# Turning the larger probability blocks of layer 1 on VectorE and by DMA, with TensorE's order tied

## The chip, the cores and the metric

The kernel runs on one core of a Trainium2 chip. A core has TensorE (PE, the matrix engine, whose weight loads the profile lists apart as PEld), VectorE (DVE), ScalarE (ACT), GpSimd (POOL) and SyncE (SP), which here issues nearly all DMAs. Each engine runs its own instructions in order and waits for the others by semaphores. The metric is the device time of one execution in microseconds (us).

## The reference

One step of a two-layer streaming encoder, on 512 prompt rows and 32 sample rows. Layer 0 is an RWKV-7 mixer, layer 1 differential attention with 12 heads of width 128; each layer has one input projection, memory attention beside the mixer, a SiLU gate and an output projection. The part that matters is layer 1's prompt attention, done for each head in four blocks of 128 queries, where a query sees the keys of its own block and of those before it:

```python
def probs(qa, ka):
    s = jnp.einsum('bqhd,bkhd->bhqk', qa, ka).astype(jnp.float32) * DF_HD ** -0.5
    return jax.nn.softmax(jnp.where(mask, s, NEG_INF), axis=-1)

attn = probs(q1, k1) - lam * probs(q2, k2)
return jnp.einsum('bhqk,bkhd->bqhd', attn.astype(v_all.dtype), v_all)
```

## The kernel before

**The projections set the beat.** All 544 rows lie turned in SBUF, split into a high and a low part (`hh`, `hl`). Each 128 columns of a weight matrix are a block: the weights arrive as two loads (`raw`), ScalarE rounds them to `whi`, VectorE takes the rest as `wlo`, and TensorE runs 48 matmuls into `ps_g`: two halves of 272 rows, eight k-parts, and for each `hh,whi`, `hl,whi`, `hh,wlo`. `block` writes these 48 in order and, ahead of the matmul with a given index, takes a step of other work. In `groups`, four heads make a group, and there are three groups; each head has a K, a Q and a V block, then gate and memory blocks follow.

**A head's steps.** `diff_head` is a generator; `groups` places its steps in its own V block, in the next head's K, Q and V blocks, and in the gate block after the fourth head. `turned(k)` and `turned(v)` turn keys and values within 32 rows on VectorE (`kt`, `vb`) and store them by DMA; `vscr` is the DRAM scratch of the values, and `fetched` loads it back in order as `vt`. `scores(t)`, for query block t, runs the `ps_s` matmuls, takes the maxima on VectorE (`snm`), the exponentials on ScalarE (`pt`) and combines both softmaxes on VectorE. `probs(t)` turns the t + 1 key blocks of `pt` on TensorE into `ps_aT`, which ScalarE copies to `aT`. `weighted(t)` multiplies `aT` with `vt` into `ps_o`, t + 1 matmuls of two passes each. `taken` copies `ps_o` to `ot` on VectorE and squares it on ScalarE. `diff_end` ends a group: the sample rows' result `ps_os`, its norm on VectorE (`os`), its turn `ps_osT` and each head's turn `ps_oT`.

**What sets the order.** The instructions are written in program order, and a scheduler then lays out each engine's order by readiness. `Queue.tie` can bind a queue's instructions to the program's order; in the kernel before it does so only in a part of layer 0 (`self.ordered`), so in layer 1 the scheduler places TensorE's instructions too.

Of the kernel before, what the change touches and what calls it, by code (L numbers as in the profile page):

```python
# [97 lines left out]
class Queue:  # L98


    def __init__(self, trunk, engine):
        self.trunk, self.engine, self.last = trunk, engine, None

    def __getattr__(self, name):
        issue = getattr(self.engine, name)
# [3 lines left out]
class Trunk:  # L109
# [12 lines left out]

    def tie(self, queue, ins):

        if self.ordered:
            if queue.last is not None:
                self.order(ins, queue.last)
            queue.last = ins
        return ins
# [1654 lines left out]
    def layer1(self):  # L1784
# [7 lines left out]
        with ExitStack() as ctx:  # L1792
            with ExitStack() as c2:
                self.dfp = p = self.pool("df", 1, ctx=c2)
                m1 = c2.enter_context(ExitStack())
                mp = self.pool("mem1a", 1, ctx=m1, side="right")

                nlam = self.nlam
                self.vscr = [self.dp.tile([TP, P], F32, name=f"vscr{i}") for i in range(2)]
                self.qs = [p.tile([P, P], F32, name=f"qs{i}") for i in range(2)]  # L1800
                for t in self.qs:
                    nc.gpsimd.memset(t[:], 0.0)  # L1802
                self.kz = [p.tile([P, 2, T], F32R, name=f"kz{i}") for i in range(2)]
                for t in self.kz:
                    for m in range(2):
                        r = slice(64 - 64 * m, P - 64 * m)
                        nc.gpsimd.memset(t[r, m, :].bitcast(F32), 0.0)
                pe, early = [], iter(order[:MADE])

                def aside():  # L1810
                    if pe:
                        made.update({g: self.gated(g, *self.fetch(pe[0], g)) for g in islice(early, 2)})

                def free():
                    m1.close()
                    pe.append(self.pool("wo1e", 1, ctx=ctx, side="right"))

                self.groups(w, p, mp, nlam, aside, free)
            p = self.pool("wo1", 1, ctx=ctx)
            fw = p.tile([P, D], F32, name="fw")  # L1820
            self.se.dma_start(fw[:], a["final_norm_w"].unsqueeze(0).to_broadcast([P, D]))
            sums = p.tile([P, T], F32, name="sums")
            ys = [p.tile([P, D], F32, name=f"fy{i}") for i in range(5)]
            rows = [P] * 4 + [TS]

            def transposed(s, pool, tag, tiles=range(5)):

                for i in tiles:
                    ps = pool[i].tile([P, 512], F32, tag=tag[i], name="ps_f")
                    for k in range(4):  # L1830
                        c = min(i * P, T - P)
                        self.te.transpose(ps[:, k * P : k * P + P], self.x1[:, 4 * s + k, c : c + P], self.ident[:])
                    yield i, slice(P - rows[i], P), ps

            def consume(k, ps, v):
                x = self.x1[:, k, v]
                if k == KT - 1:
                    cuts = (TH, 3 * P, TP, T) if v.start else (0, TH)
                    for c, e in zip(cuts, cuts[1:]):
                        x = self.x1[:, k, c:e]  # L1840
                        self.ve.tensor_tensor(x, ps[:, c - v.start : e - v.start], x, ALU.add)
                        self.ae.activation(last[:, c:e], x, AF.Square)
                    if not v.start:
                        pn.append(begun((0, 1), self.psx, "x"))
                        pn.append(begun((2, 3, 4), self.psc, "c"))
                    finish((2, 3, 4) if v.start else (0, 1))
                    return
                self.ve.tensor_tensor(x, ps, x, ALU.add)
                self.square_sums((k, x, v), p, sums)
                if k == 3 and v.start:  # L1850
                    for i, n, pf in transposed(0, [self.psm] * 5, "mmmmm"):
                        self.ve.tensor_tensor(ys[i][n, :512], pf[n, :], fw[n, :512], ALU.mult)

            last = p.tile([P, T], F32, name="last")
            rs, invd, epsd = (p.tile([P, n], F32, name=f"fr{i}") for i, n in enumerate((5, 1, 5)))
            nc.gpsimd.memset(invd[:], 1.0 / D)
            nc.gpsimd.memset(epsd[:], EPS / P)
            pn = []

            def begun(tiles, pool, tag):  # L1860

                ps = pool.tile([P, 512], F32, tag=tag, name="ps_n")
                self.te.matmul(ps[:, : len(tiles)], self.ones[:], epsd[:, : len(tiles)], start=True, stop=False)
                for j, i in enumerate(tiles):
                    c = min(i * P, T - P)
                    self.te.matmul(ps[:, j : j + 1], sums[:, c : c + P], invd[:], start=False, stop=False)
                return ps


            def finish(tiles):  # L1870

                ps = pn.pop(0)
                for j, i in enumerate(tiles):
                    c = min(i * P, T - P)
                    self.te.matmul(ps[:, j : j + 1], last[:, c : c + P], invd[:], start=False, stop=i == tiles[-1])
                v = slice(tiles[0], tiles[-1] + 1)
                self.rsqrt(rs[:, v], ps[:, : len(tiles)], p, f"tm_t{tiles[0]}")
                for i, n, pf in transposed(1, [self.psm, self.psm, self.psc, self.psm, self.psg], "mmcmg", tiles):
                    r = rs[n, i : i + 1]
                    self.ve.scalar_tensor_tensor(ys[i][n, 512:], pf[n, :], r, fw[n, 512:], ALU.mult, ALU.mult)  # L1880
                    self.ae.activation(ys[i][n, :512], ys[i][n, :512], AF.Copy, scale=r)
                    self.se.dma_start(o[0][0, i * P : i * P + P, :] if i < 4 else o[1][0], ys[i][n, :])

            for _ in self.w_out(1, p, order, consume, o=made)[0]:
                pass
# [13 lines left out]
    def groups(self, w, p, mp, nlam, aside, free):  # L1899

        late = []
        for hg in range(3):
            gr = self.diff_group(hg, p)
            heads = [self.diff_head(gr, j, p, nlam) for j in range(4)]
            sgs, fins, prev = [], [], None
            step = lambda it, *at: [(i, lambda: next(it, None)) for i in at]

            turns = lambda it, last: step(it, 6) + step(last, 8) + step(it, 20, 36) + step(last, 40) + step(it, 47)

            def gate(c0, pieces):  # L1910
                self.gates += 1
# [4 lines left out]
            for j, (parts, it) in enumerate(heads):  # L1916
                h = 4 * hg + j
                before = step(prev, 4, 14, 24, 36) if j else late
                k, q, v = parts()
                self.block(w, MIXW + h * P, k, before)  # L1920
                if not j and hg == 2:
                    free()
                next(it)
                self.block(w, h * P, q, step(prev, 4, 40) if j else ())
                if j:
                    aside()
                if j == 3 and hg < 2:
                    mem = [self.mem_turn(1, 2 * hg + i, mp) for i in range(2)]
                    for _ in range(2):
                        next(mem[0][1])  # L1930
                self.block(w, 2 * MIXW + h * P, v, turns(it, prev if j else iter(())))
                prev = it
            end = self.diff_end(gr, nlam)
            fin = lambda j, at: (at, lambda: end.send((j, sgs[j])))
            g0 = 4 * hg * P
            sgs.append(gate(g0, step(prev, 4, 14, 24, 36)))
            if hg == 2:
                sgs.append(gate(g0 + P, step(prev, 4, 28, 40, 45)))
                aside()
                sgs.append(gate(g0 + 2 * P, step(end, 2, 10, 18) + [fin(0, 22), fin(1, 36)]))  # L1940
                sgs.append(gate(g0 + 3 * P, [fin(2, 16)]))
                fin(3, 0)[1]()
                break
            (st0, m0), (st1, m1) = mem
            for st, h in ((st0, 2 * hg), (st1, 2 * hg + 1)):
# [43 lines left out]
    def diff_head(self, gr, j, p, nlam):  # L1989
# [65 lines left out]
        def probs(t):  # L2055
# [4 lines left out]
            st["aT", t] = p.tile([P, 512], F32, tag="aT", name="aT", bufs=3)  # L2060
            self.ae.copy(st["aT", t][:, :n], ps[:, :n])

        def weighted(t):
            aT = st["aT", t]
            if t == 0:
                st["po"] = self.psx.tile([P, 4, P], F32, tag="x", name="ps_o")
            for i in range(t + 1):
                self.te.matmul(st["po"][:, t, :], aT[:, i * P : i * P + P], st["vt"][:, i, :], start=i == 0, stop=i == t)

        def taken():  # L2070
            ot = st["ot"]
# [5 lines left out]
        def steps():  # L2077
# [39 lines left out]
            yield  # L2117
            scores(3)
            yield
            probs(2)  # L2120
            yield
            for t in range(3):
                weighted(t)
            self.se.dma_start(o[5][0, 0, :, h, :].rearrange("(i p) d -> p i d", p=P), st["vt"][:])
            probs(3)
            yield
            weighted(3)
            yield
# [139 lines left out]
```

## Time and profile before

| | |
|---|---|
| median of 3 runs | 1360.98 us (1359.95 to 1361.36) |
| the profiled execution, its own time | 1360.13 us |
| its span, first to last instruction | 1358.4 us |
| granted clock of TensorE, mean | 0.998 |
| DMA, mean over the span | 107 GB/s |

By stretches of the span, the first column giving start:end in us, then the length, the busy time and number of instructions of PE, PEld, DVE, ACT and POOL, the granted clock, the busy share of the DMA engines and GB/s:

```profile
712.00:797.00 85.00, 83.60 (x676) 82.44 (x674) 51.17 (x108) 37.58 (x82) 2.53 (x6) 1.00 0.57 154
797.00:1250.00 453.00, 450.67 (x3512) 437.54 (x3511) 312.61 (x862) 252.82 (x769) 6.34 (x6) 1.00 0.44 112
1250.00:1358.40 108.40, 100.26 (x804) 99.48 (x802) 46.50 (x89) 28.36 (x57) 7.02 (x4) 0.97 0.27 84
```

The heads of layer 1 fill the middle row. In a timeline a row is start, length, engine, line, operation, written tile <- read tiles, shapes and count, and in brackets the idle time before it with what ended it. Every row has line 106, a helper's, so tiles tell the rows apart. Matmuls are pipelined: a single one's length is longer than the distance between two starts.

### The profile page before, as it was taken

How to read it: one execution, taken by the hardware profiler on the slowest of the kernel's cores; microseconds unless marked ns; L12 is line 12 of the kernel's file. 1: busy time of each engine (PE TensorE's matmuls, PEld its weight loads, DVE VectorE, ACT ScalarE, POOL GpSimd, SP SyncE). 2: the span in 40 equal slices, each digit the busy share in tenths (PEclk: the TensorE clock that was granted, in tenths of full speed). 3: DMA queues.
4: the chain of work that ended last, by engine and by line, in shares of the span. 5: the costliest groups of instructions: out<-in, count | busy, mean ns of one | idle time of the engine just before them, and what ended most of it. 6: DMA issues, size and time to landing. Idle time of an engine off the chain costs nothing. (4 is left out here: it accounts for less than half of the span.)

```text
span 1358.4 us, 31641 instructions
## 1 busy us (share of the span) xinstructions
PE 1328.2 (98%) x11725; PEld 1271.8 (94%) x11725; DVE 945.2 (70%) x2373; ACT 804.1 (59%) x2252; POOL 370.4 (27%) x833
## 2 busy tenths in 40 slices
PE   8999999999999999999999999999999999999997
PEld 6988899999999998988999999999999999999997
DVE  5766778878888888666754677775577747777443
ACT  5766777877787776656433466654466536665222
POOL 2128668666776667600000000000000001002000
PEclk9999999999999999999999999999999999999999
DMA  6452322333223332432565574543354424443322
GB/s 223 144 139 68 86 59 67 85 94 82 72 81 87 79 84 65 116 107 81 160 158 144 142 200 110 130 119 93 95 127 111 113 79 108 119 107 103 94 79 73
DMA packets 330964, 145.54 MB, mean 107 GB/s; under 512 B 129865, under 2 KB 319826, under 8 KB 330810
## 3 DMA queue, kind: packets, MB, share of 16 engines
q1 hardware_dynamic: 330746, 143.51, 39.5%
q8 instruction: 92, 1.51, 0.5%
q14 instruction: 62, 0.51, 0.1%
q10 hardware_dynamic: 64, 0.02, 0.0%
HBM read 113.87 MB, written 26.06 MB: 103 GB/s over the span
## 5 line engine op out<-in xcount | busy, mean ns | idle before, releaser
L106 PE MATMUL ps_g<-hh,wlo 128*128 128x272 f32 x1808 | 537.9, 298 | 1.1 <-DVE wlo L106 1.0
L106 PE MATMUL ps_g<-hh,whi 128*128 128x272 f32 x1808 | 534.3, 296 | 0.9 <-DVE ats L106 0.7
L106 PE MATMUL ps_g<-hl,whi 128*128 128x272 f32 x1808 | 533.1, 296 | 0.9 <-DVE hl L106 0.7
L106 PEld LDWEIGHTS ps_g<-hh,whi 128*128 128x128 f32 x1808 | 341.6, 189 | 5.3 <-issue 0.9
L106 PEld LDWEIGHTS ps_g<-hl,whi 128*128 128x128 f32 x1808 | 341.3, 189 | 3.6 <-DVE hl L106 1.8
L106 PEld LDWEIGHTS ps_g<-hh,wlo 128*128 128x128 f32 x1808 | 341.2, 189 | 2.9 <-DVE wlo L106 1.8
L106 DVE TENSOR_TENSOR wlo<-raw,whi 128x512 fp32r<-128x512 f32 x314 | 213.6, 692 | 120.2 <-ACT whi L106 116.3
L106 ACT CAST whi<-raw 128x512 fp32r<-128x512 f32 x314 | 188.7, 619 | 121.4 <-PE ps_g L106 69.8
L868 POOL TENSOR_TENSOR tm<-u,m 102x84 f32<-102x84 f32 (+23 forms) x341 | 147.6, 433 | 115.8 <-DMA m<-sc 67.4
L870 POOL TENSOR_TENSOR u<-u,tm 102x84 f32<-102x84 f32 (+23 forms) x341 | 152.8, 448 | 26.6
L106 PE MATMUL ps_g<-hi,wlo 128*128 128x272 f32 x512 | 148.0, 289 | 0.9 <-DVE wlo L106 0.9
L106 PE MATMUL ps_g<-hi,whi 128*128 128x272 f32 x512 | 147.8, 289 | 0.0
L106 PE MATMUL ps_g<-lo,whi 128*128 128x272 f32 x512 | 147.6, 288 | 0.0
L1339 POOL TENSOR_TENSOR lo<-og,hi 128x544 fp32r<-128x544 f32 x8 | 13.2, 1652 | 386.0 <-ACT hi L106 385.5
L106 PEld LDWEIGHTS ps_g<-hi,wlo 128*128 128x128 f32 x512 | 96.5, 188 | 1.5 <-DVE wlo L106 1.4
L106 PEld LDWEIGHTS ps_g<-hi,whi 128*128 128x128 f32 x512 | 96.7, 189 | 0.0
L106 PEld LDWEIGHTS ps_g<-lo,whi 128*128 128x128 f32 x512 | 96.5, 188 | 0.0
L106 ACT ACTIVATE pt<-ps_s,snm 128x128 f32<-128x128 f32 (+3 forms) x96 | 50.1, 526 | 59.9 <-DVE snm L106 59.7
L106 DVE SCALAR_TENSOR_TENSOR SB<-ps_c,dl,sd 64x64 f32<-64x64 f32 x168 | 47.4, 282 | 26.4 <-PE ps_c L106 21.9
L106 ACT COPY sv<-ps_c 64x64 f32<-64x64 f32 x192 | 39.5, 206 | 32.8 <-PE ps_c L106 30.9
L1802 POOL MEMSET qs<- 128x128 f32 x2 | 0.3, 204 | 187.0 <-PE ps_g L106 187.0
L106 ACT ACTIVATE sg<-ps_g 128x272 f32<-128x272 f32 x64 | 25.2, 393 | 41.2 <-PE ps_g L106 38.2
(393 smaller groups left out, 2522.7 us busy)
## 6 DMA issues: line engine op xcount, KB each, us to landing
raw<-in_rw_in_dram SPq DMA_DIRECT2D x114, 256.0 KB
raw<-in_df_in_dram SPq DMA_DIRECT2D x112, 256.0 KB
raw<-in_w_out_dram SPq DMA_DIRECT2D x64, 256.0 KB
oscr<-sg SPq DMA_DIRECT2D x16, 272.0 KB
lo<-oscr SPq DMA_DIRECT2D x16, 272.0 KB
m<-sc SPq DMA_DIRECT2D x33, 128.0 KB
raw<-in_w_mem_v_dram SPq DMA_DIRECT2D x16, 256.0 KB
kh<-kh SPq DMA_DIRECT2D x24, 136.0 KB
```

What stands on the lines that cost most here:

```text
L106: return lambda *a, **k: self.trunk.tie(self, issue(*a, **k))
L868: nc.gpsimd.tensor_tensor(tm[:, :n, :wd], u3[:, :n, kx : kx + 1].to_broadcast(sh), m3[:, kx : kx + 1, kx + 1 :].to_broadcast(sh), ALU.mult)
L870: nc.gpsimd.tensor_tensor(u3[:, :n, kx + 1 :], u3[:, :n, kx + 1 :], tm[:, :n, :wd], ALU.add)
L1339: (self.nc.gpsimd if g % 2 and self.o1 else self.ve).tensor_tensor(lo[:], t, hi[:].bitcast(F32), ALU.subtract)
L1802: nc.gpsimd.memset(t[:], 0.0)
```

## The change

For the first three heads of each group, `probs(2)` and `probs(3)` are replaced by `moved(2)` and `moved(3)`: VectorE turns `pt` within 32 rows and 32 columns, writing with steps of 3 or 4 elements; one DMA stores the result to a DRAM scratch (`ascr`), and four DMAs load it into place, so that key block i of the result is the columns i, i + t + 1, and so on. `weighted` reads its stationary operand with that step. The fourth head keeps `probs`. Two tiles that are not yet in use in that stage (`og` 8 and 9 as output of the turn, 10 and 11 as result) hold the data. The steps move: `weighted(0)` and `(1)` now come at index 40 of the next head's Q block, `(2)` at 16 and `(3)` at 44 of its V block, `taken` at index 2 of the K block after it. TensorE's order in all three groups is tied to the program's.

```diff
-        if self.ordered:
+        if self.ordered or queue.tied:
...
+                self.ascr = [self.dp.tile([P, TP], F32, name=f"ascr{i}") for i in range(4)]
...
+        self.te.last, self.te.tied = None, True
...
-            turns = lambda it, last: step(it, 6) + step(last, 8) + step(it, 20, 36) + step(last, 40) + step(it, 47)
+            turns = lambda it, last: step(it, 6) + step(last, 16) + step(it, 20, 36) + step(last, 44) + step(it, 47)
...
                 before = step(prev, 4, 14, 24, 36) if j else late
+                if j > 1:
+                    before = step(heads[j - 2][1], 2) + before
...
-                self.block(w, h * P, q, step(prev, 4, 40) if j else ())
+                self.block(w, h * P, q, step(prev, 4, 30, 40) if j else ())
...
-            sgs.append(gate(g0, step(prev, 4, 14, 24, 36)))
+            sgs.append(gate(g0, step(heads[2][1], 2) + step(prev, 4, 14, 24, 36)))
...
+                self.te.tied = False
...
+        def moved(t):
+            n, pt, s = (t + 1) * P, st["pt", t], self.ascr[2 * (h % 2) + t - 2]
+            x, to = self.o1[6 + t][:, :n], self.o1[8 + t]
+            self.ve.transpose(x.rearrange("p (b c i) -> p b i c", b=4, c=TS),
+                              pt[:, 0, :n].rearrange("p (i b c) -> p b i c", b=4, c=TS))
+            self.se.dma_start(s[:, :n], x)
+            for b in range(4):
+                r, c = slice(TS * b, TS * b + TS), slice(n // 4 * b, n // 4 * b + n // 4)
+                self.se.dma_start(to[r, :n].rearrange("i (a w) -> i a w", a=4),
+                                  s[:, c].rearrange("(a i) w -> i a w", a=4))
+            st["aT", t] = to[:, :n].rearrange("p (q i) -> p i q", q=P)
...
-                self.te.matmul(st["po"][:, t, :], aT[:, i * P : i * P + P], st["vt"][:, i, :], start=i == 0, stop=i == t)
+                a = aT[:, i] if t > 1 and j < 3 else aT[:, i * P : i * P + P]
+                self.te.matmul(st["po"][:, t, :], a, st["vt"][:, i, :], start=i == 0, stop=i == t)
...
-            probs(2)
-            yield
-            for t in range(3):
+            if j == 3:
+                probs(2)
+                yield
+            else:
+                for t in (2, 3):
+                    moved(t)
+                    yield
+            for t in range(3 if j == 3 else 2):
                 weighted(t)
...
-            probs(3)
+            if j == 3:
+                probs(3)
+            else:
+                yield
+                weighted(2)
```

**TensorE in the first block of the first group.** The matmuls read `hl` while its last two k-parts are still being made; a wait for VectorE on a row with `hl` is the wait for such a part, one for ScalarE on a row with `hh` that for its high part. The order before:

```order
L106 MATMUL ps_g<-hh,whi 128x272 [waits Activation_49]
L106 MATMUL ps_g<-hh,whi 128x272
L106 MATMUL ps_g<-hl,whi 128x272
L106 MATMUL ps_g<-hh,wlo 128x272
L106 MATMUL ps_g<-hl,whi 128x272 [waits DVE_49]
```

and now, from the same row on:

```order
L106 MATMUL ps_g<-hh,whi 128x272 [waits Activation_49]
L106 MATMUL ps_g<-hl,whi 128x272 [waits DVE_49]
L106 MATMUL ps_g<-hh,wlo 128x272
L106 MATMUL ps_g<-hh,whi 128x272 [waits Activation_49]
L106 MATMUL ps_g<-hl,whi 128x272 [waits DVE_49]
```

The fifth row is the 797.47 us row of the trace before, where `hl`'s last part but one is read. Now it reads the last part, whose reader stood 19 rows further on.

**TensorE and VectorE around `weighted(0)` and the second head's softmaxes.** TensorE in the next head's Q block, before:

```order
L106 MATMUL ps_aT<-ident,pt 128x128 x4
L106 MATMUL ps_g<-hl,whi 128x272
L106 MATMUL ps_g<-hh,wlo 128x272
L106 MATMUL ps_o<-vt,aT 128x128 x6
L106 MATMUL ps_g<-hh,whi 128x272
```

and now:

```order
L106 MATMUL ps_g<-hh,wlo 128x272
L106 MATMUL ps_g<-hh,whi 128x272
L106 MATMUL ps_o<-vt,aT 128x128 x3
L106 MATMUL ps_g<-hl,whi 128x272
L106 MATMUL ps_g<-hh,wlo 128x272
```

`weighted(0)` comes two `ps_g` earlier in the block, with no turn ahead of it, and with three matmuls (blocks 0 and 1) instead of six. VectorE at the end of `scores(1)`'s softmax and at the start of `scores(3)`'s, one piece each of the difference:

```order
 L106 RECIPROCAL srs<-srs 128x2
 L106 TENSOR_TENSOR srs<-srs,nlam 128x1
+L106 COPY ot<-ps_o 128x512
 L106 TENSOR_SCALAR pt<-pt,srs 128x256
 L106 TENSOR_TENSOR wlo<-raw,whi 128x512
```

```order
 L106 SCALAR_TENSOR_TENSOR pt<-pt,srs 128x384
-L106 MEMSET ps_s 64x64 x2
+L106 MEMSET ps_s 64x64
+L106 STREAM_TRANSPOSE og_12308<-pt 128x4x3x32
+L106 MEMSET ps_s 64x64
 L106 TENSOR_REDUCE snm<-ps_s 128x1 x2
 L106 RECIPROCAL srs<-srs 128x2
```

The copy of the previous head's `ps_o` and the turn of block 2 (`og_12308` is its output) have entered VectorE's queue ahead of these softmaxes; for a group's first head there is no copy, and the turn stands behind the reduction. SyncE's queue there now:

```order
L106 DMA ascr_12326<-og_12308 128x384
L106 DMA out_dram<-kt 32x16x32
L106 DMA vt<-vscr_12323 128x4x128
L106 DMA raw<-in_df_in_dram 128x4x128
L106 DMA kh<-kh 64x544 x2
L106 DMA og_12310<-ascr_12326 32x4x96 x4
L106 DMA ascr_12327<-og_12309 128x512
L106 DMA out_dram<-vt 128x4x128
L106 DMA raw<-in_df_in_dram 128x4x128 x2
L106 DMA og_12311<-ascr_12327 32x4x128 x4
```

The rows with `ascr` are new: one store and four loads for each of the two blocks, the loads of block 2 behind `kh`, those of block 3 behind two `raw` loads.

**TensorE at a group's end.** `ps_osT` moves up by nine `ps_g`. Before, ahead of the first head's `ps_oT`:

```order
L106 MATMUL ps_osT<-ident,os 128x128
L106 MATMUL ps_g<-hh,wlo 128x272
L106 MATMUL ps_g<-hh,whi 128x272
L106 MATMUL ps_g<-hl,whi 128x272
L106 MATMUL ps_oT<-ident,ot 128x128 x4
```

Now twelve `ps_g` rows stand between `ps_osT` and `ps_oT`:

```order
L106 MATMUL ps_g<-hh,wlo 128x272
L106 MATMUL ps_g<-hh,whi 128x272
L106 MATMUL ps_g<-hl,whi 128x272
L106 MATMUL ps_osT<-ident,os 128x128
L106 MATMUL ps_g<-hh,wlo 128x272
```

In the third group `ps_os` moves up by nine `ps_g` as well, and `ps_osT` stands eight `ps_g` behind it.

More of the change, by code (lines that the diff above doesn't have):

```diff
@@ L101, in __init__ @@
     def __init__(self, trunk, engine):
-        self.trunk, self.engine, self.last = trunk, engine, None
+        self.trunk, self.engine, self.last, self.tied = trunk, engine, None, False
     def __getattr__(self, name):
```

## The prediction

> **What bounds the kernel now.** I read the page's busy times and the granted clock first, then busy time by stretch around the four heads of layer 1's first group, then TensorE's waits, then the chain and the timelines of one head.
>
> ```profile
> span 1358.4 us, 31641 instructions
> PE 1328.2 (98%) x11725; PEld 1271.8 (94%) x11725; DVE 945.2 (70%) x2373; ACT 804.1 (59%) x2252; POOL 370.4 (27%) x833
> PEclk9999999999999999999999999999999999999999
> 820.00:906.00 86.00, 85.48 (x669) 83.68 (x668) 62.02 (x168) 52.15 (x163) 0.00 (x0) 1.00 0.50 123
> ```
>
> TensorE (PE) is busy for 85.48 of 86 us there, at the full clock, and VectorE (DVE) for 62. So work taken off PE is worth its time, but only where nothing else is about to end last, and a new PE wait costs its full length. What comes nearest to that is in PE's waits from 795 to 1232 us (total, times, longest):
>
> ```profile
> PE ps_o L106 <- DMA vt<-vscr: 1.1, 3, 0.5
> PEld ps_o L106 <- DMA vt<-vscr: 2.2, 5, 0.7
> ```
>
> `weighted(0)`, the first `ps_o` matmul of a head, waits for `vt` in 8 of 12 heads. The next rows (PE, DVE, SyncE's queue, then the chain's prices) are the second head's way there.
>
> ```profile
> 836.52 0.28 PE L106 MATMUL ps_s<-kh,qp 128*128 128x256 f32 x1
> 839.65 0.17 DVE L106 RECIPROCAL srs<-srs 128x2 f32<-128x2 f32 x1 [0.76 <-ACT pt L106]
> 842.90 1.02 DVE L106 TENSOR_REDUCE snm<-ps_s 128x1 f32<-128x384 f32 x2
> 844.76 0.17 DVE L106 RECIPROCAL srs<-srs 128x2 f32<-128x2 f32 x1 [0.84 <-ACT pt L106]
> 846.38 1.29 DVE L106 TENSOR_REDUCE snm<-ps_s 128x1 f32<-128x512 f32 x2
> 848.64 0.17 DVE L106 RECIPROCAL srs<-srs 128x2 f32<-128x2 f32 x1 [0.98 <-ACT pt L106]
> 849.05 0.71 DVE L106 STREAM_TRANSPOSE kt<-k 128x512 f32<-128x512 f32 x1
> 849.79 0.32 SPq L106 DMA_DIRECT2D out_dram<-kt  x1
> 850.29 0.38 SPq L106 DMA_DIRECT2D vt<-vscr  x1
> 853.24 1.41 PEld L106 LDWEIGHTS ps_o<-vt,aT 128*128 128x128 f32 x12 [0.20 <-DMA vt<-vscr]
> 848.05 4.51 PE ps_g L106 x36
> 852.56 0.44 PE ps_aT L106 x4
> 853.25 1.59 PE ps_o L106 x12
> ```
>
> `scores(1)` starts at 836.52. The `vt` load is issued at 850.29 (13.77 us later), because SyncE issues in order and the `kt` store ahead of it waits for DVE's turn of `kt` at 849.05, which stands behind both softmaxes. PE starts `ps_o` at 853.24: 2.95 us after the issue, 16.72 us after `scores(1)`, with 0.20 us of wait. So PE's work between `scores(1)` and `weighted(0)` is already as short as the `vt` load allows. Prices: `ps_g` 4.51/36 = 0.125 us, a transpose 0.44/4 = 0.11, a `ps_o` matmul (two passes, twelve rows for six) 2 × (1.59 - 0.20)/12 = 0.23.
>
> **The transposes.** Nine heads lose 3 + 4 of them: 63 × 0.11 = 6.9 us of PE work. Every one stood ahead of `weighted(0)`, in the stretch that `vt` already sets. So I don't book the 6.9; I work out the head instead.
>
> **The heads.** For the second and third head of a group PE would now reach `weighted(0)` at 16.72 - 0.20 (wait) - 0.77 (seven transposes) - 0.25 (it moves two `ps_g` forward) + 0.93 (the four `ps_o` of the head before, which now follow `scores(1)`) = 16.43 us after `scores(1)`. The `vt` issue moves the other way. Between the two reciprocals at 839.65 and 844.76 DVE idles only 0.84 us, and that idle follows the reduction; into this stretch comes the copy of `ot`:
>
> ```profile
> L106 DVE COPY ot<-ps_o x12: 684/692/693, 833.8 to 1229.9; 128x512 f32<-128x512 f32 x12
> L106 DVE STREAM_TRANSPOSE kt<-k 128x512 f32<-128x512 f32 x12 | 8.5, 710 | 0.4
> L106 DVE STREAM_TRANSPOSE new<-k 128x32 f32<-128x32 f32 x12 | 2.5, 212 | 0.4
> ```
>
> That is 0.69. Beside it the K block itself starts 0.93 later after `scores(1)`, and with it the copy of `v` that DVE's `vb` needs; the two overlap, and I take 0.9. Then `moved(2)` stands between the memsets ahead of the reduction at 846.38: a turn of 384 columns, between 212 ns at 32 and 710 at 512, is 0.58 by straight line. Reduction, exponentials, `kt`, its store and `vt` follow in one chain, so the issue comes 1.5 later, at 15.27, and `vt` lands at 18.22: PE waits 1.8 us. Its start moves by 18.22 - 16.72 = +1.50. Behind it, up to the next `scores(1)`, six instead of ten `ps_o` matmuls and two more `ps_g` stand: -0.93 + 0.25 = -0.68. Each of the two heads: +0.82.
>
> The group's first head has no `ot` copy, and its `moved(2)` falls into the 0.98 us idle at 848.64, so its `vt` is not later:
>
> ```profile
> 825.27 0.38 SPq L106 DMA_DIRECT2D vt<-vscr  x1
> 828.56 1.50 PE L106 MATMUL ps_o<-vt,aT 128*128 128x128 f32 x12
> 897.19 0.46 SPq L106 DMA_DIRECT2D vt<-vscr  x1
> 902.67 1.50 PE L106 MATMUL ps_o<-vt,aT 128*128 128x128 f32 x12
> ```
>
> PE can start at 825.27 + 2.95 = 828.22 instead of 828.56: -0.34 - 0.68 = -1.02. In the fourth head the third's four `ps_o` come on top (+0.93); there `ps_o` came 5.5 us after the issue, so no wait forms. A group: -1.02 + 2 × 0.82 + 0.93 = +1.55; three groups **+4.7 us**.
>
> **The tied order, first block.** PE can no longer pass `hl` parts that are late:
>
> ```profile
> 797.47 0.40 PE L106 MATMUL ps_g<-hl,whi 128*128 128x272 f32 x1 [0.32 <-DVE hl L106]
> 798.36 0.65 ACT L106 CAST hh<-hn 128x544 fp32r<-128x544 f32 x1
> 799.04 0.72 DVE L106 TENSOR_TENSOR hl<-hn,hh 128x544 fp32r<-128x544 f32 x1 [0.80 <-ACT hh L106]
> ```
>
> Before, the matmul that uses the last `hl` stood 19 rows behind the one at 797.47 (19 × 0.125 = 2.4 us). Now it has that one's own row, and `hl` is ready at 799.76 whatever PE does: **+2.3 us**.
>
> **The tied order, `ps_osT`.** It moves nine `ps_g` (1.13 us) forward in each group; in the last group `ps_os` does too, and `ps_osT` stands eight `ps_g` behind it.
>
> ```profile
> 913.95 0.29 DVE L106 TENSOR_SCALAR os<-os,os 128x128 f32<-128x128 f32 x1
> 914.39 0.30 PE L106 MATMUL ps_osT<-ident,os 128*128 128x128 f32 x1
> 1076.41 0.30 PE L106 MATMUL ps_osT<-ident,os 128*128 128x128 f32 x1 [0.21 <-DVE os L106]
> 1233.48 0.16 PEld L106 LDWEIGHTS ps_os<-cv,aTs 128*32 128x32 f32 x8 [0.18 <-ACT aTs L106]
> 1237.22 0.75 DVE L106 SCALAR_TENSOR_TENSOR og<-ps_oT,dv,sg 128x512 f32<-128x512 f32 x1
> 1237.88 0.29 DVE L106 TENSOR_SCALAR os<-os,os 128x128 f32<-128x128 f32 x1
> ```
>
> DVE's rows up to `os` are the same in the first two groups. There `os` is done at 914.24 where PE would come at 913.26: +1.0; the second waited already: +1.1. In the third `ps_os` waited already (+1.1), and `os` is done at 1238.17 less the 0.66 of the `og` row that now follows it, 1237.5, where PE comes at 1233.5 + 0.7 + 8 × 0.125 = 1235.2: +2.3; grouped transposes and an earlier `ps_o` give back some 0.5. **+5.0 us.**
>
> **What costs nothing, and its cover.** ScalarE's 18 `aT` copies fall away; nobody waited for them. The `og` loads of `moved(2)` stand on SyncE's queue behind `kh`:
>
> ```profile
> 851.32 1.10 SPq L106 DMA_DIRECT2D kh<-kh  x2
> L106 SPq DMA_DIRECT2D vs<-new x12: 599/608/736, 894.3 to 1220.5; - x12
> ```
>
> With `kh` 1.5 later the four go out from 853.9 to 856.4 (0.61 each, like `vs`). None carries more than a fifth of `vt`'s bytes, so the last lands within `vt`'s 2.95 us of its issue at 855.8, by 858.7; `weighted(2)` comes 24 `ps_g` and three `ps_o` after `weighted(0)` at 854.7, at 858.4. I take no wait, for the smaller load; at worst 0.3 × 9 = 2.7 us. `raw` loads queue some 3 us later but feed blocks two further on (12 us). `moved(3)`'s turn (0.71) and the second `kt` stores hide behind PE's wait. A strided write could make `moved(2)` up to twice as long (+0.58 × 6 = +3.5) and not shorter than a plain turn; I take the plain row, the same instruction.
>
> **The sum.** 4.7 + 2.3 + 5.0 = +12.0 us on the profiled execution's 1360.13 us: 1372.1. The median of the runs is 0.85 above that execution, so 1373.0 (+0.9%).
>
> **Rivals.**
>
> *The weight loads get slow.* `weighted(2)` and `(3)` now read their stationary operand in steps of 12 and 16 bytes; nothing in the trace reads so. Nearest row:
>
> ```profile
> L106 PEld LDWEIGHTS ps_o<-vt,aT x240: 186/192/193, 828.4 to 1229.5; 128*128 128x128 f32 x120
> ```
>
> Nine heads × 7 matmuls × 2 passes = 126 passes of 0.116; at twice that, +14.6: 1387.6. Bounds 0 and 14.6; I take 0, as plain rows cost. It decides from a load that no longer fits under the matmul ahead. The Trainium skill, page "SBUF — State Buffer", section "Door 1: The DMA port swizzle", says that SBUF has 16-byte lines and needs two accesses to a line for full bandwidth, yet also calls a stride of four fp32 free: the first would make this rival true, the second not. No row here shows which.
>
> *DVE's delay does not reach `vt`.* Then a group is -1.02 - 2 × 0.68 + 0.93 = -1.45, the sum -4.4 + 7.3 = +3.0: 1364.0. Against it: DVE has no idle left ahead of 846.38.
>
> *Faster: `vt` is in time.* If `vt` were issued by 16.43 - 2.95 = 13.48 us after `scores(1)`, the 6.9 us and the 3.3 us of present waits would go: -10.2 + 7.3 = -2.9, 1358.1. It needs 0.3 us less than the trace's 13.77, where I count 1.5 more.
>
> **Numbers.** The forecast 0.57 (1366 to 1380), slow loads 0.17, no delay 0.15, faster 0.06, something else 0.05. The range 1362 to 1388 leaves out the faster case, part of the third and the far end of the first. A change under 0.2% (2.7 us) is about what a measurement of this kernel can't tell from none: faster 0.07; within, half of the no-delay case and some of the rest, 0.10; slower 0.83.
>
> **What would show it.** Right: PE and PEld waits of `ps_o` on `vt` of 1 to 2 us in two heads of three; one wait of about 2.3 us of `ps_g` on `hl` near 798 us; waits of `ps_osT` on `os` of 1, 1 and 2.3; `ps_aT` down to 57. Wrong: `vt` issued no later after `scores(1)`, waits of `ps_o` on `og`, or `ps_o` rows much apart where nothing is waited for.

## The result, and the profile after

The changed kernel takes 1385.51 us (median of 6 runs, 1382.39 to 1387.31) where the kernel before takes 1361.42 (1359.95 to 1361.92): a ratio of 1.0176 with a 95% interval of 1.0163 to 1.0189, or +24.1 us. The forecast was slower by 12.0, at 1373.0. The direction held; the size was half of what came.

The page of the kernel after (profiled execution 1387.31 us), and TensorE's waits over the span (total, times, longest):

```profile
span 1385.6 us, 31645 instructions
PE 1338.9 (97%) x11662; PEld 1281.0 (92%) x11662; DVE 962.8 (69%) x2391; ACT 796.3 (57%) x2234; POOL 371.1 (27%) x833
```

```profile
PE ps_o L106 <- DMA vt<-vscr: 8.6, 9, 1.5
PE ps_osT L106 <- DVE os L106: 4.8, 3, 2.4
PE ps_g L106 <- ACT hh L106: 1.6, 1, 1.6
PE ps_g L106 <- DVE hl L106: 1.2, 3, 0.7
PE ps_os L106 <- ACT aTs L106: 1.1, 1, 1.1
PE ps_o L106 <- DMA og<-ascr: 0.6, 2, 0.3
```

TensorE has 63 matmuls fewer and yet is busy 10.7 us longer. The waits stand where the prediction put them: `vt` (in nine heads; it named two of every three), `ps_osT` three times, `hl` and its high part `hh` in the first block; the short ones for `og` are new. They explain the idle time, not the busy time. That comes from two other rows. First, `ps_o` by its stationary operand (ns min/median/max of one):

```profile
L106 PEld LDWEIGHTS ps_o<-vt,og x126: 251/319/332, 839.8 to 1234.7; 128*128 128x128 f32 x126
L106 PEld LDWEIGHTS ps_o<-vt,aT x114: 186/192/192, 836.1 to 1251.7; 128*128 128x128 f32 x114
```

Read in steps of 12 and 16 bytes (`og`), a load takes 251 to 332 ns, read plainly (`aT`) 186 to 192. Second, the clock in the first block and at the third group's end (by stretches; the granted clock is the third column from the end):

```profile
800.00:802.00 2.00, 0.99 (x6) 0.54 (x4) 1.94 (x4) 0.23 (x1) 0.00 (x0) 1.00 0.91 270
802.00:804.00 2.00, 0.59 (x1) 0.28 (x1) 0.68 (x1) 1.16 (x3) 0.00 (x0) 0.84 0.84 258
804.00:806.00 2.00, 1.90 (x8) 1.90 (x9) 0.04 (x1) 0.39 (x1) 0.00 (x0) 0.50 0.76 208
806.00:808.00 2.00, 2.00 (x15) 2.00 (x14) 0.00 (x0) 0.00 (x0) 0.00 (x0) 0.80 0.77 270
...
1258.00:1260.00 2.00, 0.00 (x0) 0.00 (x0) 2.00 (x15) 0.00 (x0) 0.00 (x0) 1.00 0.37 107
1260.00:1262.00 2.00, 1.97 (x12) 2.00 (x13) 1.69 (x9) 0.37 (x1) 0.00 (x0) 0.69 0.00 0
1262.00:1264.00 2.00, 2.00 (x11) 2.00 (x10) 1.38 (x5) 0.40 (x1) 0.00 (x0) 0.50 0.00 0
```

TensorE idles, and just behind the idle time it runs at half clock: 8 or 11 matmuls in 2 us instead of some 16 (669 in 86 us before). PE's timeline in the first block, and the row of the third end that waits:

```profile
801.18 0.40 PE L106 MATMUL ps_g<-hl,whi 128*128 128x272 f32 x1 [0.71 <-DVE hl L106]
...
803.34 0.59 PE L106 MATMUL ps_g<-hh,whi 128*128 128x272 f32 x1 [1.64 <-ACT hh L106]
804.10 0.59 PE L106 MATMUL ps_g<-hl,whi 128*128 128x272 f32 x1 [0.17 <-DVE hl L106]
804.49 0.43 PE L106 MATMUL ps_g<-hh,wlo 128*128 128x272 f32 x1
804.72 0.43 PE L106 MATMUL ps_g<-hh,whi 128*128 128x272 f32 x1
...
806.90 0.29 PE L106 MATMUL ps_g<-hl,whi 128*128 128x272 f32 x1
807.03 0.29 PE L106 MATMUL ps_g<-hh,wlo 128*128 128x272 f32 x1
...
1260.03 0.30 PE L106 MATMUL ps_osT<-ident,os 128*128 128x128 f32 x1 [2.39 <-DVE os L106]
```

Starts are 0.23 us apart from 804.49 on and 0.13 again behind 806.90. The trace's record of the granted clock has 3.41 us at 0.5 there, worth 1.7 us, and as much behind 1260.03.

**Where the 27.2 us lie.** The two spans differ by 27.2. The start of the same instruction in both traces, subtracted, gives how far the kernel after lags at each place:

| stretch | before grows by |
|---|---|
| up to the first block of the groups (793.76 us before, 797.46 after) | +3.7 |
| first block, up to the first `scores` (16.07 us before, 20.21 after) | +4.1 |
| heads of the three groups | +4.4, +4.4, +3.7 |
| the three group ends | +1.1, +1.0, +4.5 |

The first row isn't the change's: up to there no engine's order differs, and in the 15 further profiles below that block starts between 791.8 and 795.1. In this execution a stretch of 6.83 us at half clock, at 131 us, makes 3.4 of it. The other rows, 23.2 in all, come near the 24.1 between the medians.

The first head's `ps_o`, and then the second head, as in the prediction's rows:

```profile
836.08 0.94 PE L106 MATMUL ps_o<-vt,aT 128*128 128x128 f32 x6 [0.55 <-DMA vt<-vscr]
843.89 0.28 PE L106 MATMUL ps_s<-kh,qp 128*128 128x256 f32 x1
845.88 2.10 PE L106 MATMUL ps_o<-vt,og 128*128 128x128 f32 x8 [0.34 <-DMA og<-ascr]
855.20 0.69 DVE L106 STREAM_TRANSPOSE og<-pt 128x384 f32<-128x384 f32 x1
859.72 0.36 SPq L106 DMA_DIRECT2D vt<-vscr  x1
862.82 0.94 PE L106 MATMUL ps_o<-vt,aT 128*128 128x128 f32 x6 [1.06 <-DMA vt<-vscr]
866.63 1.19 PE L106 MATMUL ps_o<-vt,og 128*128 128x128 f32 x6
872.10 2.01 PE L106 MATMUL ps_o<-vt,og 128*128 128x128 f32 x8
```

`vt` is issued 15.83 us after `scores(1)` (13.77 before) and `ps_o` starts at 18.93 (16.72 before). The eight strided passes of `weighted(3)` take 2.01 us, so 0.23 each, (2.01 - 0.40)/7; the six plain ones of 862.82 0.11, (0.94 - 0.38)/5; the six of `weighted(2)` at 866.63 0.16, (1.19 - 0.40)/5.

### The profile page after: what moved, and what is told of

It is laid out like the page before. It is cut to its first block, busy times and chain, and to the rows that moved or that the text cites. A ratio compares the mean times of both kernels' runs of the same rounds, so it can differ in the third digit from the quotient of the medians.

```text
span 1385.6 us, 31645 instructions
## 1 busy us (share of the span) xinstructions
PE 1338.9 (97%) x11662; PEld 1281.0 (92%) x11662; DVE 962.8 (69%) x2391; ACT 796.3 (57%) x2234; POOL 371.1 (27%) x833
```

## The experiments

Two theories stood against each other. The first: the tie makes new waits, these bring the clock down, and strided weight loads are slow. The second, the prediction's own sum: waits alone. The times below stand against the kernel before on the same chip, with 95% intervals of the ratio.

**One part alone: the tie.**

```diff
-        if self.ordered:
+        if self.ordered or queue.tied:
...
+        self.te.last, self.te.tied = None, True
         for hg in range(3):
```

> The kernel before, with TensorE's order tied to the program's in the three groups and nothing else; turns, copies and the steps' places are those of before. Theory: the tie alone makes TensorE idle some 2.3 us in the first block, and the granted clock then falls to 0.5 for 3.4 us (+1.8); ps_osT waits +1.1 and +1.0 at the first two group ends; at the third +2.9 and again a 3.4 us stretch at half clock (+1.7); ps_o stands two ps_g earlier and waits up to 0.25 longer for vt in nine heads (0 to 2.2). In all +10.8 to +13.0 us: 1372 to 1374.5, ratio 1.008 to 1.0095, mean clock near 0.995. Rival: the two half-clock stretches belong to something else in the change; then +7.3 to +9.5 (1368.5 to 1371) and a clock of 0.998.

Measured: 1376.59, ratio 1.0116 (1.0101 to 1.0131), +16.2: above both. First block 19.86 us (+3.8), group ends +1.1, +1.1, +4.5, each as in the full change, with two half-clock stretches. The heads add 1.8, 1.9 and 2.1, where up to 2.2 in all was expected:

```profile
PE ps_o L106 <- DMA vt<-vscr: 5.7, 8, 1.1
856.71 1.60 PE L106 MATMUL ps_o<-vt,aT 128*128 128x128 f32 x12 [0.80 <-DMA vt<-vscr]
858.15 0.60 PE L106 MATMUL ps_aT<-ident,pt 128*128 128x128 f32 x4
```

TensorE waits 5.7 us for `vt` where it waited 1.1 before, because less work stands ahead of `weighted(0)` and `vt` comes no earlier. Two `ps_g` (0.25 us) and the four turns of `probs(3)` (0.44), which the scheduler had laid ahead of it, now follow it: 0.69 in each of nine heads would be 6.2, and 5.8 came. The changed kernel has no `probs(3)` in these heads, so most of this part belongs to the kernel before; what the two have in common are the 10.5 us in the first block and at the ends.

**One part alone: the strided reading.**

```diff
+            if t > 1 and j < 3:
+                a = st["aT", t][:, :n].rearrange("p (q i) -> p i q", q=P)
+                self.ae.copy(a, ps[:, :n].rearrange("p (i q) -> p i q", q=P))
...
+                a = aT[:, i] if t > 1 and j < 3 else aT[:, i * P : i * P + P]
```

> The kernel before, but ScalarE writes aT of blocks 2 and 3 interleaved and weighted reads it in steps of 12 and 16 bytes, in the first three heads of each group; no instruction changes its place. Theory: the weight loads themselves are slow. A pass takes 0.16 us at 12 bytes and 0.23 at 16 where a plain one takes 0.11: 54 x 0.05 + 72 x 0.12 = 11.3 us, of which the present waits for vt (3.3 us) can absorb some 2.5 where weighted(3) stands ahead of the next head's weighted(0): +8.8 to +11.3, 1370 to 1373, ratio 1.0065 to 1.0083; weight loads of 250 and 320 ns. Rival: the loads are slow only because DMA traffic or the source tile makes them so; then 188 ns and +0 to +1.

Measured: 1366.80, ratio 1.0046 (1.0031 to 1.0061), +6.4. No engine's order differs, and the loads are as slow as in the change:

```profile
L106 PEld LDWEIGHTS ps_o<-vt,aT x240: 186/253/332, 827.6 to 1235.1; 128*128 128x128 f32 x120
```

The cause is shown: the step itself, not the DMAs or the tile. A group's first head grows by 1.3 us, as the spacing says (6 x 0.05 + 8 x 0.12); the second and third by 0.3 to 0.9, because waits, gone from this trace, gave up the rest: those of `ps_o` for `vt`, and 2.2 us of the weight loads of `ps_s` for `pt`. More was absorbed than expected, 4.9 of 11.3.

**The change without the tie.**

```diff
-        self.te.last, self.te.tied = None, True
```

> The change with TensorE's order left to the scheduler. Theory: what the tie costs (4.1 in the first block, 2.1 at two group ends, 4.6 at the third) comes back, -10.8 us: 1374 to 1376 (ratio 1.010 to 1.011), no half-clock stretch in or after the first block, and the waits of ps_o for vt stay within 2 us of 8.6. Rival: left alone, the scheduler places ps_s and ps_o elsewhere and loses as much in the heads: 1383 or more.

Measured: 1381.97, ratio 1.0158 (1.0141 to 1.0175), between the two. The first block is whole again (16.15 us), and the loss moves, not into the heads, as the rival had it, but to the group ends, where new waits come:

```profile
PE ps_oT L106 <- DVE ot L106: 6.7, 4, 2.8
PE ps_g L106 <- ACT whi L106: 2.0, 2, 1.0
```

By the same lag the heads now grow by 0.0, 0.4 and -3.4 us and the ends by 6.1, 6.5 and 12.3, in part work that the scheduler pushed there from the heads. No wait of `ps_o` for `vt` is left, where the theory kept 8.6, and a stretch of 6.83 us at half clock stands at the third end.

**The tie in the heads alone.**

```diff
                 self.block(w, MIXW + h * P, k, before)
+                if not j:
+                    self.te.last, self.te.tied = None, True
...
+            self.te.tied = False
             end = self.diff_end(gr, nlam)
```

> The change, with TensorE tied only from the end of a group's first K block to the end of its fourth head, so that the first block and the group ends have the scheduler's order again (hl and ps_osT where they stood before). Theory: the heads keep their +12 to +13, the rest goes: -3.7 to -4.1 in the first block with its half-clock stretch, -2.2 at two group ends, -4.5 at the third with its stretch: 1374.5 to 1376 (ratio 1.010 to 1.011), clock 0.998. Rival: as with no tie at all, the group ends wait for ot instead and the time stays above 1380.

Measured: 1371.98, ratio 1.0086 (1.0072 to 1.0100), 13.5 below the change (12.2 by the ratios): more than expected, and of the expected kind. First block 16.06, no half-clock stretch, the first group's end +0.0; the heads keep 11.3 of the lag. So the first block and the ends are the tie's, and removing it there gives them back.

**Is it the clock? TensorE kept busy in the stalls.** Transposes of the identity ahead of the late matmuls:

```diff
+                    before = [(19, lambda: fill(6)), (21, lambda: fill(14))]
...
-step(end, 2, 10, 18)
+step(end, 2, 10) + [(17, lambda: fill(20))] + step(end, 18)
```

> The change, with transposes of the identity that nobody reads put on TensorE in the stalls of the tied order: 6 and 14 of them ahead of the first block's last hl and hh, 20 ahead of the third group's ps_osT; they should fit into idle time of 0.7, 1.6 and 2.4 us. Theory: TensorE idles in these stalls, and that is why the clock falls; kept busy, it stays at full clock in both places and the two stretches of 3.4 us at half clock go: -3.4 to -3.6, 1381.5 to 1382.5 (ratio 1.015), two half-clock stretches fewer, the waits themselves as late as before. Rival: the clock falls for another reason; then both stretches stay and the time is 1385 or a little more.

Measured: 1383.63, ratio 1.0175 (1.0161 to 1.0189). No half-clock stretch is left in either place; the third end costs +3.0 instead of +4.5. In the first block the transposes waited 1.45 us for their buffer and then ran past the stall (19.3 us), so that part stayed open. Again, with a free buffer and 5 and 7 transposes:

```diff
-                    before = [(19, lambda: fill(6)), (21, lambda: fill(14))]
+                    before = [(19, lambda: fill(5)), (21, lambda: fill(7))]
```

> The change with transposes of the identity in the stalls, from a buffer that is free there: 5 ahead of the first block's last but one hl, 7 ahead of its last hh, 20 ahead of the third group's ps_osT. Theory: no half-clock stretch in either place; the first block takes 17.8 to 18.5 us up to the first scores instead of 19.8 to 20.2 (16.1 in the scheduler's order), the third end +3.0 instead of +4.5. Rival: the block stays at 19.5 or more, so the clock isn't what its second half cost.

Measured: 1383.02, ratio 1.0168 (1.0152 to 1.0183). The first block takes 18.44 us, the third end +3.0, and the clock stays up:

```profile
797.00:800.00 3.00, 2.29 (x16) 1.85 (x17) 1.32 (x3) 1.38 (x4) 0.00 (x0) 1.00 0.88 268
800.00:803.00 3.00, 3.00 (x26) 3.00 (x26) 0.00 (x0) 0.51 (x2) 0.00 (x0) 1.00 0.73 243
...
1257.00:1260.00 3.00, 3.00 (x27) 3.00 (x26) 2.45 (x7) 0.40 (x1) 0.00 (x0) 1.00 0.00 0
1260.00:1263.00 3.00, 3.00 (x27) 3.00 (x26) 1.71 (x4) 1.42 (x3) 0.00 (x0) 1.00 0.02 5
```

In these two places useless work on a waiting engine saves about 3 us (1.4 to 1.8, and 1.5); over the whole kernel the intervals of the ratios overlap. That the clock follows TensorE's idle time is shown by the places.

**`vt` earlier, in the kernel before.** On SyncE's queue the `kt` stores are held behind `vt`:

```diff
+                if n == 4 and self.vtl is not None:
+                    self.order(s, self.vtl)
```

> The kernel before, with the kt stores held behind the vt load on SyncE's queue. Theory: the present waits of ps_o for vt go, which are 1.1 us on TensorE and 2.2 on its weight loads: -1.1 to -3.3, 1357 to 1359.3 (ratio 0.9976 to 0.9992). Rival: vt is bounded by the vscr stores or its buffer; no change.

Measured: 1357.94, ratio 0.9983 (0.9974 to 0.9992): as expected, and faster than both kernels. With `vt` early the scheduler itself lays `weighted(0)` ahead of the turns of `probs(3)`, so TensorE's order differs too. The same by another way, the load issued by GpSimd:

```diff
-            self.se.dma_start(t[:], self.vscr[h % 2][:].rearrange("(i p) d -> p i d", p=P))
+            self.nc.gpsimd.dma_start(t[:], self.vscr[h % 2][:].rearrange("(i p) d -> p i d", p=P))
```

> The kernel before, with the vt load issued by GpSimd instead of SyncE. Theory: as with the kt stores held behind it, the waits of ps_o for vt go: -1.5 to -3, 1357 to 1358.7 (ratio 0.9978 to 0.999). Rival: GpSimd issues later than SyncE did; 1360 or more.

Measured: 1357.67, ratio 0.9980 (0.9971 to 0.9989). GpSimd issues the second head's `vt` 5.6 us before SyncE did (850.29; 1.8 of it are this trace's lead), and no wait for it is left:

```profile
844.65 0.76 POOL L2034 DMA_DIRECT2D vt<-vscr  x1 [24.52 <-DMA vscr<-vb]
```

**`vt` earlier, in the change.** First with the `kt` and the `ascr` stores held behind it on SyncE:

```diff
+                if n == 4 and self.vtl is not None:
+                    self.order(s, self.vtl)
...
-            self.se.dma_start(s[:, :n], x)
+            self.order(self.se.dma_start(s[:, :n], x), self.vtl)
```

> The change, with the kt stores and the ascr stores held behind the vt load of the head before them on SyncE's queue; TensorE's order is the same instruction for instruction. Theory: vt is late only because SyncE waits for VectorE's turns ahead of it; the vscr stores are out some 6 us earlier. With vt issued 3 to 4 us earlier the 8.6 us of waits of ps_o for vt go, og comes at most 1 us later: -6 to -8.6, 1377 to 1379.5 (ratio 1.012 to 1.014). Rival: the og blocks, pushed back on the queue, become the wait (more than 0.5 us in most heads): 1383 or more.

Measured: 1407.27, ratio 1.0344 (1.0328 to 1.0360). A clear miss: worse than the change by 22. SyncE's queue in the third head shows why:

```profile
879.29 7.51 SPq L106 DMA_DIRECT2D raw<-in_df_in_dram  x2
886.90 0.47 SPq L106 DMA_DIRECT2D kh<-kh  x1
887.55 0.45 SPq L106 DMA_DIRECT2D vt<-vscr  x1
```

```profile
PE ps_o L106 <- DMA og<-ascr: 12.5, 7, 3.7
PE ps_o L106 <- DMA vt<-vscr: 11.1, 3, 3.7
```

With the new constraint the scheduler put `vt` behind two `raw` loads, which hold the queue for 7.5 us, and behind a `kh`; TensorE waits 3.7 us for `vt` in each third head and 12.5 in all for `og`, and the clock falls eight times. By GpSimd, with the edit shown above; on SyncE's queue a few DMAs at the group ends change places:

> The change, with the vt load issued by GpSimd, which is idle in these heads, instead of SyncE; SyncE's queue is otherwise the same and TensorE's order is the same. Theory: vt is late only because of what stands ahead of it on SyncE's queue; issued when the vscr stores have landed, 3 to 4 us earlier, it takes the waits of ps_o for vt (8.6 us) away. TensorE then reaches weighted(2) up to 1 us earlier and waits for og 0.3 to 0.7 in some heads: -4 to -8, 1377.5 to 1381.5 (ratio 1.0125 to 1.0155). Rival: vt is bounded by its data or by GpSimd's issue; the waits stay and the time is 1384 or more.

Measured: 1380.00, ratio 1.0144 (1.0130 to 1.0157), a time as expected. The 8.6 us of waits for `vt` are gone and the `og` blocks are late next, by up to 1.1 us where 0.3 to 0.7 was expected:

```profile
PE ps_o L106 <- DMA og<-ascr: 6.5, 11, 1.1
```

**Plain blocks in the change.** First by the DMAs: VectorE writes runs of 32, four stores with runs of 128 bytes, four loads of whole rows.

```diff
-            self.ve.transpose(x.rearrange("p (b c i) -> p b i c", b=4, c=TS),
-                              pt[:, 0, :n].rearrange("p (i b c) -> p b i c", b=4, c=TS))
-            self.se.dma_start(s[:, :n], x)
+            self.ve.transpose(x.rearrange("p (b i c) -> p i b c", b=4, c=TS),
+                              pt[:, 0, :n].rearrange("p (i b c) -> p i b c", b=4, c=TS))
+            flat = s[:].rearrange("p n -> (p n)")[: P * n]
+            for a in range(4):
+                self.se.dma_start(flat.rearrange("(r m a c) -> a r m c", r=TS, a=4, c=TS)[a],
+                                  x[TS * a : TS * a + TS, :].rearrange("r (m c) -> r m c", c=TS))
```

> The change, but its data are placed so that weighted reads plain 128-column blocks: VectorE writes runs of 32 elements, four stores put them in runs of 128 bytes into the scratch, four loads bring whole rows of 1.5 or 2 KB back. TensorE's order is that of the change; on SyncE's queue the kt store now stands behind the vt load. Theory: passes of weighted(2) and (3) fall back to 0.11 us, -11.3; where weighted(3) stands ahead of a wait for vt, the wait takes up to 0.96 of it in six heads, unless vt comes earlier by the queue: in all -5.5 to -11.3, 1374 to 1380 (ratio 1.0095 to 1.0135); VectorE's turns take 0.58 and 0.71 instead of 0.69 and 1.10. Rival: eight DMAs with 128 byte pieces make the blocks land late; ps_o waits for og more than 1 us in most of nine heads and the time is 1385 or more.

Measured: 1412.57, ratio 1.0386 (1.0370 to 1.0401). The loads of `ps_o` are at 192 ns again, so the slow passes are cured, at a price of 27 us on top of the change:

```profile
PE ps_o L106 <- DMA vt<-vscr: 22.3, 6, 4.0
```

The scheduler again moved `vt` behind `raw` and `kh`, so this run doesn't tell the cost of the small pieces from that of the queue. Then by a copy on GpSimd, `weighted(2)` and `(3)` somewhat later:

```diff
+            self.nc.gpsimd.tensor_copy(aT[:, :n].rearrange("p (i q) -> p i q", q=P),
+                                       to[:, :n].rearrange("p (q i) -> p i q", q=P))
```

> The change, with each og block copied by GpSimd into plain 128-column blocks before weighted reads it; weighted(2) and (3) come 12 and 2 ps_g later in the V block to leave time for the copy. Theory: the passes fall back to 0.11 us. Of the 11.3 us of slow passes the waits for vt take up to 0.96 in six heads, as in the kernel before, where reading in steps cost 6.4: -5 to -7, 1378.5 to 1380.5 (ratio 1.0135 to 1.015). Rival: the copy (1.65 us for 544 columns on GpSimd elsewhere in the trace) comes too late and ps_o waits for aT: 1383 or more.

Measured: 1383.69, ratio 1.0171 (1.0157 to 1.0185): the rival.

```profile
864.61 0.70 POOL L2079 COPY aT<-og 128x384 f32<-128x384 f32 x1 [19.21 <-DMA og<-ascr]
869.64 1.12 POOL L2079 COPY aT<-og 128x512 f32<-128x512 f32 x1 [4.33 <-DMA og<-ascr]
...
PE ps_o L106 <- POOL aT L2079: 7.7, 8, 2.0
```

The copy itself is short, but it starts when `og` has landed, and TensorE waits 7.7 us for copies in eight places.

**All cures together:** the edits of the tie in the heads, of `vt` by GpSimd and of the copies, with `weighted(2)` and `(3)` at 28 and 46.

```diff
-step(it, 6) + step(last, 16) + step(it, 20, 36) + step(last, 44) + step(it, 47)
+step(it, 6) + step(it, 20) + step(last, 28) + step(it, 36) + step(last, 46) + step(it, 47)
```

> The change with three cures: TensorE tied only in the heads, the vt load issued by GpSimd, and the og blocks copied by GpSimd into plain blocks with weighted(2) and (3) 12 and 2 ps_g later. Theory: from the 1372 of the tie in the heads alone, the waits for vt (8.5) and the slow passes (6 to 11) go, some waits for og or its copies come: 1353 to 1359, ratio 0.995 to 0.999, faster than before; the 63 transposes then pay for the first time. Rival: the way over the scratch and GpSimd is too long; ps_o waits for the copies 1 us a head and the time is 1362 or more.

Measured: 1368.73, ratio 1.0061 (1.0048 to 1.0073): the rival, with 12.1 us of waits for the copies. With `weighted(3)` 2.6 us later:

```diff
-                    before = step(heads[j - 2][1], 2) + before
+                    before = sorted(step(heads[j - 2][1], 20, 22) + before, key=lambda s: s[0])
```

> The run with three cures (TensorE tied in the heads alone, vt by GpSimd, og blocks copied by GpSimd), and weighted(3) with the copy of ot moved from the V block's end to 20 and 22 of the next K block, 2.6 us later on TensorE. Theory: what is left in that run are 12.1 us of waits for the copies and two stretches of 3.4 us at half clock that follow them; with both gone 1353 to 1356, ratio 0.9945 to 0.997, so that the 63 transposes pay 2 to 5 us against the 1357.7 of the kernel before with vt by GpSimd. Rival: the removed transposes are worth nothing, since the late ot and block 2's copies become the next wait: 1358 or more.

Measured: 1367.89, ratio 1.0055 (1.0042 to 1.0067): the rival again. Up to the third head's first `scores` this kernel gets 3.0 us ahead of the one before; the 14 missing transposes (1.5) and `weighted(2)`, which comes later (0.7), make 2.2 of it, so the transposes do pay where nothing is late. Then `weighted(2)` of the second head waits 3.1 us (4.3 in the third group), because the scheduler laid the `og` loads of block 2 behind block 3's store:

```profile
850.61 3.60 SPq L106 DMA_DIRECT2D ascr<-og  x2
...
855.40 3.83 SPq L106 DMA_DIRECT2D og<-ascr  x8
```

The same without the copies:

> As the run before, but without the copies: weighted reads og in steps of 12 and 16 bytes, as in the change. Theory: with no wait left for the slow passes to eat into, they cost their full 54 x 0.05 + 72 x 0.12 = 11.3 us on top of that run, instead of the 6.4 measured beside waits: 1363 to 1368. Rival: 6 or less; the passes hide under the matmuls ahead of them.

Measured: 1372.23, ratio 1.0082 (1.0069 to 1.0096), 4.3 above the run before it. That is the rival's time, but not for its reason: the strided passes still take 0.20 us on average, as in the change. The waits for `og` (7.5) are 4.7 us smaller than that run's for the copies (12.2), so 9.0 is an estimate of what the passes cost there; their full price showed as lost time only in the first heads of the strided reading alone (1.3 each), not over a kernel. No version with the moved blocks was found that beats the kernel before; that one could be, with SyncE's queue laid out by hand, was not tried.

## Why the prediction was right and wrong

- **The first block, forecast +2.3, measured +4.1.** The stall has the size worked out, 0.71 + 1.64 + 0.17 us of waits for 0.32 before, 2.2, though in three waits, the longest for `hh`, and not in one for `hl`. The step that failed is "a new PE wait costs its full length", and no more: behind it came 1.7 us at half clock. The trace of before has its clock at 1.00 in every stretch of the heads and at half only behind TensorE's last matmul (0.51 from 1352 us on), so it put no price on a stall in between; nothing in the sum left room for it.
- **The group ends, forecast +1.0, +1.1 and +2.9 (1.1 + 2.3 - 0.5); measured +1.1, +1.0 and +4.5.** The waits came out as forecast (1.19, 1.18, 2.39); the third's excess is again 1.7 us of half clock, which the two fillers remove (+3.0).
- **The heads, forecast +4.7, measured +12.5.** This is the mis-sized term. The chain was right: the `ot` copy and `moved(2)` ahead of the reduction, `kt` and `vt` later, 15.83 us after `scores(1)` for a forecast of 15.27, `ps_o` at 18.93 for 18.22; in the first head `ps_o` starts 0.32 us earlier (forecast 0.34) by the lag there. The step that failed is "I take 0, as plain rows cost" for the strided loads: 54 passes of 0.05 us more and 72 of 0.12 are 11.3. The forecast's own waits come to 12.8 (in each group 0.77 + 0.25 - 0.34 in the first head, then 1.8 twice), and 12.8 - 1.1 (before) - 6.9 (transposes) is its +4.7 within 0.1. Measured waits of `ps_o` are 9.2 (8.6 for `vt`, 0.6 for `og`): 9.2 - 1.1 - 6.9 + 11.3 = 12.5. So the slow passes cost 11.3, and waits smaller than forecast gave back 3.6. That the step makes the passes slow is shown by the strided reading alone; that they cost this much here is counted from rows, since no run has the change with plain blocks and the same queues. The two `ps_g` by which `weighted(0)` moves were in the sum (+0.25 a head), and the four turns behind most of the tie's 5.8 in the heads of the kernel before are gone here. With 7.8 more in the heads and 3.4 of half clock the forecast's 12.0 becomes 23.2.
- **The rival with slow weight loads** (chance 0.17, 1387.6) was true in its mechanism, and too dear at 14.6: the passes cost 11.3, less 3.6 of waits. That the time fell within 2.1 us of it is luck in part: the half clock's 3.4 us, which it didn't have, came on top.
- **The faster rival** asked for `vt` in time. Given that (by GpSimd), the change gains 5.5, not 15, because the `og` blocks, "no wait" in the sum at the old pace, become the next one. It also counted the present waits twice. PE's three for `vt` stand in heads of PEld's five, so 5 of 12 heads wait and not 8, and some 2.2 us can go, not 3.3; the two runs of the kernel before with `vt` early gained 2.2 and 2.7.
- **Small terms.** `moved(2)`'s turn takes 0.69 for a forecast of 0.58, `moved(3)`'s 1.10 for 0.71: the strided write has a price, within the bound given. The waits for `og` in the change are 0.6 us, forecast none, and `ps_aT` fell to 57.

## What to carry to other kernels

On an engine at 98%, sum what a change does to each wait separately and ask what comes next when one goes: here `vt`, then `og`, then its copies, and a cure on one queue in order moved the next load behind it. Price a new stall of some 1.7 us or more at its length plus the half-clock stretch that can follow it, and keep a tensor that is read as weights in runs of plain columns unless a run has shown that the step is free. The kernel before became faster by 0.2% with one line, the critical load issued by an engine that had nothing to do.

## What the runs showed of the hardware

- **Strided weight loads.** A pass whose stationary operand is read in steps of 12 bytes takes 0.16 us and of 16 bytes 0.23, instead of 0.11; the loads' own rows go from 186-192 to 251 and 319-332 ns. The Trainium skill, page "SBUF — State Buffer", section "Door 1: The DMA port swizzle", says both that two accesses to a 16-byte line are needed for full speed and that four fp32 elements can be strided for free. The first agrees with these rows; the second does not, and the measurement decides.
- **The clock.** In the kernel after, up to the third group's end, the stretches at half clock lie behind idle time of TensorE (and one, at 131 us, behind 1.1 us of waits among 32 x 32 matmuls), last 3.41 or 6.83 us, and their starts within one execution are whole multiples of 3.413 us apart (672.4 and 457.4 us, 197 and 134 times). The Trainium skill, page "TensorE: Matmul & The Clock Gate", section "What's actually happening", states a window of 3413 ns that runs freely; the trace agrees with the length and the grid. Its section "HAM oscillation — how this bites in real kernels" gives the rule of no idle gaps above some 3.4 us; here 2.39 us at the third end were enough, and 2.35 in two pieces in the first block, while a gap of 2.70 us (the tie in the heads alone, at 1022.64 us) and all gaps of 1.0 to 1.5 us for `vt` in the change stayed without it.
- **Where the gap lies on the grid.** The grid can be laid over each of the 17 traces from its own half-clock starts. Between 780 and 1310 us 39 windows at full clock come just ahead of half clock, and in 36 of them TensorE's rows, overlaps counted once, fill less than half (in the other three 53, 58 and 63%); of the 2531 other windows at full clock one is that empty (48%). With the windows moved half a length earlier or later only 12 or 18 of the 39 are. The gap of 2.39 us lies within one window, which is 30% filled; the one of 2.70 us lies across an edge, and its two windows are 67 and 54% filled. One gap of 1.76 us was enough (the last run above, at 1028.74 us). So a gap shorter than a window costs its length, or its length and 1.7 us more, by how it falls on the grid. This is read from the traces; no run moved a gap on purpose.
- **Copies on GpSimd.** From steps of 12 and 16 bytes to plain columns, 128 rows: 0.70 us for 384 columns, 1.1 for 512.
